# One more pair by seven products, the split ahead of the loop, the gate rows and the last norm of a two-layer fp32 encoder trunk

## The chip, the core and the metric

The kernel runs on one core of a Trainium2 chip. The metric is device microseconds of one execution, less is better; a measured kernel is run several times and its median is given. Five engines with instruction queues of their own work on it: TensorE (PE, with its weight loads as PEld), VectorE (DVE), ScalarE (ACT), GpSimd (POOL) and SyncE (SP). Here SP issues nearly all weight loads, POOL some other transfers. Each engine takes its instructions in program order; between engines they wait for semaphores.

## The reference

Two post-norm layers on x of 256 positions by 2048 columns, all in float32. The first layer mixes by a gated MLP (gMLP), the second by attention with a low-rank query and key/value; each is followed by a gated MLP with a causal convolution. What the change touches is the gMLP and the last norm:

```
def gmlp_mixer(x, w_in, ln_g, ln_b, w_s, b_s, w_out):
    z = jax.nn.gelu(x @ w_in)
    u, v = jnp.split(z, 2, axis=-1)
    v = layer_norm(v, ln_g, ln_b)
    v = v.reshape(B, S // GM_BLOCK, GM_BLOCK, GM_GROUPS, GM_GROUP_DIM)
    ...
    s = jnp.einsum('gij,bnjgd->bnigd', w, v) + jnp.transpose(b_s)[None, None, :, :, None]
    return (u * s.reshape(B, S, GM_HALF)) @ w_out
...
    for i in range(DEPTH):
        ...
        x = layer_norm(ALPHA * x + m, ln_mix_g[i], ln_mix_b[i])
        f = conv_ffn(x, ffn_w_up[i], ffn_conv_w[i], ffn_conv_b[i], ffn_w_down[i])
        x = layer_norm(ALPHA * x + f, ln_ffn_g[i], ln_ffn_b[i])
```

layer_norm is (x - mean) / sqrt(var + eps) * g + b over a row.

## The kernel before

**Products.** float32 products are made of three matmuls each (L236): an operand is split into a high part (rounded to the format fp32r) and a low part (the rest), and high x high, low x high and high x low are added up in PSUM. The x parts are split once at the start (`xhl`). A weight chunk is 128 rows (k) of 2048 columns (1 MB): SP loads it into one of three `raw` slots, ACT casts its high part `wh` (L131), DVE subtracts to get the low part `wl` (L134). The parts stand in 14 `big` slots, of which the x parts hold 6. `Feed` keeps this going: it has so many chunks split ahead of PE's use, and loads two further ones.

**Eight and seven products.** A group of outputs is 256 rows (two halves b) by 1024 columns (two halves f), in four PSUM banks. A chunk holds two k blocks of 1024 columns. Normally it takes eight products of 128x128x512, 24 matmuls (`Banks.eight`). A chunk can also be done by seven products, 21 matmuls (`Banks.seven`), as in a Strassen scheme: DVE makes sums `ts` of the chunk's quarters (L141), which are split too (`th`, `tl`), and `combine` makes sums of the x parts (`turn`, L296 to L299, then the hi cast on ACT, L307, and the lo on DVE, L308). Such a pair needs eight banks, named q3, p2, e, q4 (DIRECT) and p1, q5, p7, p6 (OWN), and five big slots instead of two. After the last pair by seven of a group, `Banks.rest()` (L447 to L451) puts the four OWN banks together: one ACT copy and four DVE additions; four more (L755) add that to DIRECT.

**Stages.** V: six groups of eight chunks, in the order V_PAIRS; V_SEVEN lists the pairs by seven. GELU follows each group, and `stats` (L713) takes squares of the result with a running sum, into throw-away tiles of the pool t2 (5 slots). Then V is normalised: the mean, variance and reciprocal root (L775 to L780, L357, L359), and `norm_v`, two DVE operations for each tile of 128x512 (L796 with g, L797 with b). The rows of g and b, called gate rows, come in by `row_v` (L788): POOL asks for a broadcast of one row from a small DRAM buffer `gbrows`, into t2 tiles `vr`, whose numbers are the group, the half and 0 for g or 1 for b. That buffer is written after group 0 from a transpose on PE (L762). U follows, six groups in the same way with banks `ub`, and the spatial product of normalised V (`spatial`, unsplit fp32 matmuls) is made between its chunks. The out-projection, the norm, the MLP, the attention layer and the last MLP come after it.

**The last norm.** The output of the last down-projection arrives in four pieces of 512 columns for each half b. `Norm.piece` adds a piece (L661 before it) and takes its statistics (L664), `start` aggregates (L669) and makes the reciprocal root (L357 on ACT, L359), and `scale` runs two DVE operations for each piece (L678: minus the mean, times g; L679: times the root, plus b) and stores it (L680).

**Order.** The Tile framework's scheduler decides the order in which each engine's instructions stand; calls marked `keep_in_program_order` keep theirs. PSUM has eight banks that are handed out in turn, and a bank or a slot is given on when its last reader is done. In `order` rows below, a tile's name ends in a running number.

Of the kernel before, what the change touches and what calls it, by code (L numbers as in the profile page):

```python
# [8 lines left out]
F32 = mybir.dt.float32  # L9
# [3 lines left out]
ALU = mybir.AluOpType  # L13
AX = mybir.AxisListType

P = 128
# [4 lines left out]
NG = 8  # L21
# [15 lines left out]
C_GMG = 0  # L37
# [11 lines left out]
V_PAIRS = [[0, 1, 2, 3, 4, 5, 6, 7]] + [[0, 2, 1, 3, 5, 4, 6, 7]] * 5  # L49
V_SEVEN = [()] + [(2, 3, 4, 6)] * 5  # L50

# [164 lines left out]
def trunk(ctx: ExitStack, tc: tile.TileContext, x, xT, gm_in, gm_wout, ffn_up, ffn_dn,  # L216
# [94 lines left out]
    for j in range(4):  # L311
        t = slot([P, 4, S], f"xraw{j}", tag="side")

        def load(q):
            nc.sync.dma_start(t[:, q, :], xT[j, :, q, :])

        def split(q):
            hi = xhl[j][:, q, 0:S]
            nc.scalar.copy(hi, t[:, q, :])
            nc.vector.tensor_tensor(xhl[j][:, q, S : 2 * S], t[:, q, :], hi.bitcast(F32), ALU.subtract)  # L320

        if j == 0:

            feed.between = [lambda: load(slice(1, 2)), lambda: split(slice(1, 2))]
            load(slice(0, 1))
            feed.ahead(1, 0)
            load(slice(2, 3))
            load(slice(3, 4))
            split(slice(0, 1))
            feed.ahead(1, 1)  # L330
            split(slice(2, 3))
            split(slice(3, 4))
        else:
            load(slice(0, 2))
            load(slice(2, 4))
            feed.ahead(2 * j, 2 * j)
            split(slice(0, 2))
            split(slice(2, 4))
        xraw.append(t)
        feed.ahead(2 * j + 2, 2 * j + 1)  # L340

# [255 lines left out]
    class Norm:  # L597
# [74 lines left out]
        def scale(self, b, f):  # L672
# [7 lines left out]
            nc.sync.dma_start(out[b * P : (b + 1) * P, c], r)  # L680

        def put(self, b, f):
            i = self.idx
# [22 lines left out]

    def stats(gi):
        if gi == 0:
            nc.vector.tensor_scalar(vc, vsum[:, :, 0], -1.0 / 512, None, op0=ALU.mult)
        for b in range(2):  # L710
            for f in range(2):
                sq = tp.tile([P, 512], F32, tag="t2", name=f"vsq{gi}{b}{f}", bufs=T2)
                nc.scalar.activation(sq, v[gi][:, b, f * 512 : (f + 1) * 512], AF.Square, bias=vc[:, b : b + 1],  # L713
                                     accum_out=vsq[:, b, 2 * gi + f : 2 * gi + f + 1])
# [5 lines left out]
    for gi in range(6):  # L720

        acc = Banks(f"v{gi}", DIRECT if gi == 0 else OWN + DIRECT if gi % 2 else DIRECT + OWN)
        rest = (None,) * 4
        for c, p in enumerate(V_PAIRS[gi]):
            a = [[x_parts(xhl, 2 * p + j, b) for j in range(2)] for b in range(2)]
            got = feed.next()
            if p in V_SEVEN[gi]:
                acc.seven(a, xc[p], *got)
                if p == V_SEVEN[gi][-1]:
                    rest = acc.rest()  # L730
            else:
                acc.eight(a, *got)
            if gi == 0 and p in V_SEVEN[1]:
                x4 = xraw[p // 2]
                room = xc_room[len(xc) // 2][:, len(xc) % 2, :]
                xc[p] = combine(p, room, x4[:, 2 * (p % 2)], x4[:, 2 * (p % 2) + 1])
            if c == 2 and gi > 0:
                stats(gi - 1)
            if c == 4 and gi == 0:
                nc.sync.dma_start(cst, consts)  # L740
# [17 lines left out]
        v.append(vt)  # L758
        if gi == 0:
            lnt, bst, gbt = bank("lnrowT"), bank("brT"), bank("gbT")  # L760
            bank("spare")
            nc.tensor.transpose(gbt[0:96, 0:P], cst[:, C_GMG : C_GMG + 96], ident)  # L762
            nc.tensor.transpose(lnt[:, 0:P], lnrow, ident)
            nc.tensor.transpose(bst[:, 0:NG], brow[0:NG, :], ident[0:NG, 0:NG])
            gbs = tp.tile([P, P], F32, tag="t1", name="gbs", bufs=T1)
            nc.scalar.copy(gbs[0:96, :], gbt[0:96, 0:P])
            nc.gpsimd.dma_start(gbd.rearrange("r (f c) -> (r f) c", c=P), gbs[0:96, :])
            nc.scalar.copy(lncol, lnt[:, 0:P])
            nc.scalar.copy(bsc, bst[:, 0:NG])
    stats(5)  # L770
    mv = [st.tile([P, 4], F32, tag="vmv", name=f"vmv{b}", bufs=2) for b in range(2)]
# [10 lines left out]

    def row_v(g, f):

        got = []
        for i in range(2):
            t = tp.tile([P, 512], F32, tag="t2", name=f"vr{g}{f}{i}", bufs=T2)
            nc.gpsimd.dma_start(t, gbd[12 * i + 2 * g + f : 12 * i + 2 * g + f + 1, :].to_broadcast([P, 512]))  # L788
            got.append(t)
        return got  # L790

    def norm_v(g, f, rows):
# [5 lines left out]

    for f, rows in enumerate([row_v(0, 0), row_v(0, 1)]):
        norm_v(0, f, rows)  # L800

    pT = [t.rearrange("p b (f c) -> p f b c", c=P) for t in v]
    acts = Acts(pT, "wo", NF_GM)
    ub = [bank(f"ub{i}") for i in range(8)]

    def spatial(g, tiles):
# [413 lines left out]
    for b in range(2):  # L1220
        for f in (2, 3):
            end(b, f)
            ln.piece(b, f, acc[b][f])
        ln.start(b)
        for f in range(4):
            ln.scale(b, f)
# [85 lines left out]
```

## Time and profile before

| | |
|---|---|
| three runs | 2468.65, 2469.26, 2470.97 us (median 2469.26) |
| the profiled execution | 2471.25 us, its span 2469.5 us |
| mean granted TensorE clock | 0.998 |
| busy in the span: PE, DVE, ACT, POOL | 2453.7, 2054.2, 1459.5, 104.2 us |
| V, U and the way between them | PE starts at 4.7 us; the first group of U has its last product at 304.6 us |
| end of the last matmul | 2459.0 us |

The page of a profile names each group of instructions by the line of the kernel, the engine, the operation, the output and its inputs, and gives counts, busy time and the idle time before them with what ended it. A timeline gives single instructions: start, duration, and in brackets the idle time of that engine before it. Matmuls are pipelined, so a row of PE lasts longer than the step from one to the next; steps are taken between starts. A row with x2 is two instructions that follow each other.

### The profile page before, as it was taken

To read this page: it belongs to the slowest core of one execution; us is meant where nothing else is said; L and a number is where in the kernel's file an instruction comes from. 1 tells how busy PE (TensorE), PEld (TensorE's weight loads), DVE (VectorE), ACT (ScalarE), POOL (GpSimd) and SP (SyncE) were. 2 spreads that over 40 slices of the span, in tenths; PEclk is the share of its full clock that TensorE was granted. 3 is DMA by queue.
4 is the path that set the end of the run, shared out by engine and by line. 5 is a ranking of instruction groups with operands and counts; after the bars stand their busy time and mean duration, and the time that the engine had idled before them with its cause. 6 is when DMAs were issued, how large, how long until landed. Compare 5 with 4: busy or idle time off the path is not lost. (4 is left out here: it accounts for less than half of the span.)

```text
span 2469.5 us, 32459 instructions
## 1 busy us (share of the span) xinstructions
PE 2453.7 (99%) x12481; PEld 2091.0 (85%) x12481; DVE 2054.2 (83%) x2734; ACT 1459.5 (59%) x1969; POOL 104.2 (4%) x202
## 2 busy tenths in 40 slices
PE   9999999999999999999999999999999999999998
PEld 7888788888888888888888888988888888888886
DVE  7999899889898788788777897867598787878798
ACT  6666565566565666556655566665565665655453
POOL 0000000000000000000000000000000000000000
PEclk9999999999999999999999999999999999999999
DMA  7555766656665678777868885544478787877885
GB/s 276 204 205 208 231 204 194 217 181 213 206 219 190 230 291 322 297 279 288 330 215 320 303 300 184 193 158 161 172 270 310 273 312 294 300 264 274 300 324 201
DMA packets 117004, 611.94 MB, mean 248 GB/s; under 512 B 10712, under 2 KB 11488, under 8 KB 75760
## 3 DMA queue, kind: packets, MB, share of 16 engines
q1 hardware_dynamic: 90704, 462.47, 52.7%
q0 software_dynamic: 26144, 147.39, 15.9%
q8 instruction: 98, 1.61, 0.3%
q14 instruction: 58, 0.48, 0.1%
HBM read 544.75 MB, written 65.06 MB: 247 GB/s over the span
## 5 line engine op out<-in xcount | busy, mean ns | idle before, releaser
L134 DVE TENSOR_TENSOR wl<-raw,wh 128x1024 fp32r<-128x1024 f32 (+4 forms) x645 | 957.3, 1499 | 176.8 <-ACT wh L131 131.8
L131 ACT CAST wh<-raw 128x1024 fp32r<-128x1024 f32 (+4 forms) x645 | 809.3, 1278 | 362.6 <-PE up L236 85.7
L236 PE MATMUL up<-xhl,wh 128*128 128x512 f32 x2624 | 611.4, 390 | 0.0
L236 PEld LDWEIGHTS up<-xhl,wh 128*128 128x128 f32 x2624 | 487.5, 188 | 97.7
L236 PEld LDWEIGHTS up<-xhl,wl 128*128 128x128 f32 x2624 | 325.8, 192 | 6.4
L236 PE MATMUL up<-xhl,wl 128*128 128x256 f32 x2624 | 328.1, 283 | 0.0
L131 ACT CAST th<-ts 128x1536 fp32r<-128x1536 f32 (+1 forms) x138 | 142.8, 1052 | 113.8 <-DVE ts L141 89.4
L236 PE MATMUL ub<-wh,xhl 128*128 128x512 f32 x576 | 179.5, 393 | 1.9 <-DVE u0w L449 1.9
L134 DVE TENSOR_TENSOR tl<-ts,th 128x1536 fp32r<-128x1536 f32 (+1 forms) x138 | 162.9, 1217 | 10.5 <-ACT th L131 3.6
L236 PEld LDWEIGHTS ub<-wh,xhl 128*128 128x128 f32 x576 | 108.1, 188 | 26.4 <-DVE u0w L449 2.4
L236 PE MATMUL ub<-wl,xhl 128*128 128x512 f32 x288 | 112.2, 389 | 0.0
L141 DVE TENSOR_TENSOR ts<-ts,raw 128x512 f32<-128x512 f32 x138 | 94.5, 684 | 1.4
L141 DVE TENSOR_TENSOR ts<-raw 128x1024 f32<-128x1024 f32 x69 | 84.0, 1218 | 7.7 <-PE ub L236 3.8
L236 PE MATMUL mo<-wh,oT 128*128 128x512 f32 x256 | 82.5, 401 | 0.0
L236 PE MATMUL v_q<-wh,xhl 128*128 128x512 f32 x224 | 70.1, 394 | 1.7 <-ACT wh L131 1.7
L236 PEld LDWEIGHTS ub<-wl,xhl 128*128 128x128 f32 x288 | 54.1, 188 | 11.4
L236 PE MATMUL v_p<-wh,xhl 128*128 128x512 f32 x192 | 60.2, 392 | 0.1
L236 PEld LDWEIGHTS v_q<-wh,xhl 128*128 128x128 f32 x224 | 42.2, 190 | 11.3 <-ACT wh L131 2.7
L236 PEld LDWEIGHTS mo<-wh,oT 128*128 128x128 f32 x256 | 45.5, 189 | 7.1
L236 PE MATMUL mo<-wl,oT 128*128 128x512 f32 x128 | 50.1, 392 | 0.0
L693 ACT ACTIVATE lny<-lnt,lncol 128x128 f32<-128x128 f32 x96 | 36.5, 469 | 15.7 <-PE lnt L689 15.6
L396 DVE TENSOR_TENSOR h_0a<-up,lo_0a 128x256 f32<-128x256 f32 x41 | 17.2, 419 | 32.7 <-ACT lo_0a L394 32.7
(1826 smaller groups left out, 4328.4 us busy)
## 6 DMA issues: line engine op xcount, KB each, us to landing
raw<-in_ffn_up_dram SPq DMA_DIRECT2D x172, 1024.0 KB, 7.1
raw<-in_gm_in_dram SPq DMA_DIRECT2D x93, 1024.0 KB, 5.3
raw<-in_ffn_dn_dram SPq DMA_DIRECT2D x68, 1024.0 KB, 6.9
raw<-in_gm_wout_dram SPq DMA_DIRECT2D x48, 1024.0 KB, 5.2
praw<-in_ffn_dn_dram POOLq DMA_DIRECT2D x16, 1024.0 KB, 15.2
keptth<-pth POOLq DMA_DIRECT2D x16, 1024.0 KB, 8.1
kepttl<-ptl POOLq DMA_DIRECT2D x16, 1024.0 KB, 9.0
fth<-keptth POOLq DMA_DIRECT2D x16, 1024.0 KB, 10.0
```

The lines of the kernel that those rows point to most:

```text
L131: cast = self.nc.scalar.copy(hi, raw)
L134: self.nc.vector.tensor_tensor(lo, raw, hi.bitcast(F32), ALU.subtract)
L141: add = lambda o, a, b: self.nc.vector.tensor_tensor(o, a, b, ALU.add)
L236: recent[0] = nc.tensor.matmul(o, l, r, start=start, stop=stop, skip_group_check=True)
L396: nc.vector.tensor_tensor(h, acc[:, 0:S], lo, ALU.add)
L693: nc.scalar.activation(y[:, j], t[:, j * P : (j + 1) * P], AF.Identity, bias=lncol[:, o : o + 1], scale=lncol[:, g : g + 1])
```

## The change

Four edits, in the order of the program:

1. Pair 6 of group 0 in V is by seven products (V_SEVEN). Six chunks are split ahead of the loop and seven loaded, instead of seven and eight. The x combinations for the pairs 2, 3, 4 and 6 are made ahead of the chunk instead of after it, 6 along with 4. Group 0 takes eight banks.
2. The three transposes (of the gate rows and of two other parameter tables) move from the end of group 0 to after the first chunk of group 1, into the bank p6 of that group.
3. The four DMAs of rows0 (g and b of the first two tiles) are issued ahead of the last `stats`, whose squares now go to PSUM banks of U that are not in use yet instead of t2 tiles.
4. The last norm of the second half has pieces 0 to 2 multiplied by g in advance (`weigh`); `finish` adds b and -mean * root * g on TensorE in three banks, by a product of ident with b and one of a diagonal matrix with g, and one DVE operation for each of these pieces remains. Piece 3 is as before.

```diff
@@ -47,7 +47,7 @@
 
 
-V_SEVEN = [()] + [(2, 3, 4, 6)] * 5
+V_SEVEN = [(6,)] + [(2, 3, 4, 6)] * 5
@@ -333,11 +333,11 @@
         else:
             load(slice(0, 2))
             load(slice(2, 4))
-            feed.ahead(2 * j, 2 * j)
+            feed.ahead(2 * j, min(2 * j, 6))
             split(slice(0, 2))
             split(slice(2, 4))
         xraw.append(t)
-        feed.ahead(2 * j + 2, 2 * j + 1)
+        feed.ahead(min(2 * j + 2, 7), min(2 * j + 1, 6))
 
@@ -679,6 +679,34 @@
             nc.vector.scalar_tensor_tensor(r, r, self.rs, self.b[:, c], ALU.mult, ALU.add)
             nc.sync.dma_start(out[b * P : (b + 1) * P, c], r)
 
+        def weigh(self, b, f):
+
+            r = self.r(b, f)
+            tc.keep_in_program_order(nc.vector.tensor_tensor(r, r, self.g[:, f * 512 : (f + 1) * 512], ALU.mult))
+
+        def finish(self, b):
+
+            t = [bank(f"fin{f}") for f in range(3)]
+            c = [slice(f * 512, (f + 1) * 512) for f in range(4)]
+            for f in range(3):
+                mm(t[f], ident, self.b[:, c[f]], True, False)
+            self.start(b)
+            pin = tc.keep_in_program_order
+            off = st.tile([P, 1], F32, tag="rstd", name="off")
+            pin(nc.vector.scalar_tensor_tensor(off, self.mu, -1.0, self.rs, ALU.mult, ALU.mult))
+            dg = tp.tile([P, P], F32, tag="t1", name="dg", bufs=T1)
+            pin(nc.vector.tensor_scalar(dg, ident, off, None, op0=ALU.mult))
+            for f in range(3):
+                mm(t[f], dg, self.g[:, c[f]], False, True)
+            r = self.r(b, 3)
+            pin(nc.vector.scalar_tensor_tensor(r, r, self.mu, self.g[:, c[3]], ALU.subtract, ALU.mult))
+            pin(nc.vector.scalar_tensor_tensor(r, r, self.rs, self.b[:, c[3]], ALU.mult, ALU.add))
+            nc.sync.dma_start(out[b * P : (b + 1) * P, c[3]], r)
+            for f in range(3):
+                r = self.r(b, f)
+                nc.vector.scalar_tensor_tensor(r, r, self.rs, t[f], ALU.mult, ALU.add)
+                nc.sync.dma_start(out[b * P : (b + 1) * P, c[f]], r)
+
@@ -704,12 +732,12 @@
     vsq = st.tile([P, 2, 12], F32, tag="vsq", name="vsq", bufs=1)
     vc = st.tile([P, 2], F32, tag="vc", name="vc", bufs=1)
 
-    def stats(gi):
+    def stats(gi, junk=None):
         if gi == 0:
             nc.vector.tensor_scalar(vc, vsum[:, :, 0], -1.0 / 512, None, op0=ALU.mult)
         for b in range(2):
             for f in range(2):
-                sq = tp.tile([P, 512], F32, tag="t2", name=f"vsq{gi}{b}{f}", bufs=T2)
+                sq = junk[2 * b + f] if junk else tp.tile([P, 512], F32, tag="t2", name=f"vsq{gi}{b}{f}", bufs=T2)
                 nc.scalar.activation(sq, v[gi][:, b, f * 512 : (f + 1) * 512], AF.Square, bias=vc[:, b : b + 1],
                                      accum_out=vsq[:, b, 2 * gi + f : 2 * gi + f + 1])
 
@@ -719,23 +747,34 @@
     gbd = dram.tile([24, 512], F32, tag="gbrows", name="gbrows", bufs=1)
     for gi in range(6):
 
-        acc = Banks(f"v{gi}", DIRECT if gi == 0 else OWN + DIRECT if gi % 2 else DIRECT + OWN)
+        acc = Banks(f"v{gi}", OWN + DIRECT if gi % 2 else DIRECT + OWN)
         rest = (None,) * 4
         for c, p in enumerate(V_PAIRS[gi]):
             a = [[x_parts(xhl, 2 * p + j, b) for j in range(2)] for b in range(2)]
             got = feed.next()
+            for p2 in V_SEVEN[1] if gi == 0 else ():
+                if p == {2: 2, 3: 3, 4: 4, 6: 4}[p2]:
+                    x4 = xraw[p2 // 2]
+                    room = xc_room[len(xc) // 2][:, len(xc) % 2, :]
+                    xc[p2] = combine(p2, room, x4[:, 2 * (p2 % 2)], x4[:, 2 * (p2 % 2) + 1])
             if p in V_SEVEN[gi]:
                 acc.seven(a, xc[p], *got)
                 if p == V_SEVEN[gi][-1]:
                     rest = acc.rest()
             else:
                 acc.eight(a, *got)
-            if gi == 0 and p in V_SEVEN[1]:
-                x4 = xraw[p // 2]
-                room = xc_room[len(xc) // 2][:, len(xc) % 2, :]
-                xc[p] = combine(p, room, x4[:, 2 * (p % 2)], x4[:, 2 * (p % 2) + 1])
             if c == 2 and gi > 0:
                 stats(gi - 1)
+            if c == 0 and gi == 1:
+                t = acc.acc["p6"]
+                nc.tensor.transpose(t[0:96, 0:P], cst[:, C_GMG : C_GMG + 96], ident)
+                nc.tensor.transpose(t[:, P : 2 * P], lnrow, ident)
+                nc.tensor.transpose(t[:, 2 * P : 2 * P + NG], brow[0:NG, :], ident[0:NG, 0:NG])
+                gbs = tp.tile([P, P], F32, tag="t1", name="gbs", bufs=T1)
+                nc.scalar.copy(gbs[0:96, :], t[0:96, 0:P])
+                nc.gpsimd.dma_start(gbd.rearrange("r (f c) -> (r f) c", c=P), gbs[0:96, :])
+                nc.scalar.copy(lncol, t[:, P : 2 * P])
+                nc.scalar.copy(bsc, t[:, 2 * P : 2 * P + NG])
...
@@ -756,18 +795,18 @@
...
-        if gi == 0:
-            lnt, bst, gbt = bank("lnrowT"), bank("brT"), bank("gbT")
-            bank("spare")
-            nc.tensor.transpose(gbt[0:96, 0:P], cst[:, C_GMG : C_GMG + 96], ident)
-            nc.tensor.transpose(lnt[:, 0:P], lnrow, ident)
-            nc.tensor.transpose(bst[:, 0:NG], brow[0:NG, :], ident[0:NG, 0:NG])
-            gbs = tp.tile([P, P], F32, tag="t1", name="gbs", bufs=T1)
-            nc.scalar.copy(gbs[0:96, :], gbt[0:96, 0:P])
-            nc.gpsimd.dma_start(gbd.rearrange("r (f c) -> (r f) c", c=P), gbs[0:96, :])
-            nc.scalar.copy(lncol, lnt[:, 0:P])
-            nc.scalar.copy(bsc, bst[:, 0:NG])
-    stats(5)
+    def row_v(g, f):
+
+        got = []
+        for i in range(2):
+            t = tp.tile([P, 512], F32, tag="t2", name=f"vr{g}{f}{i}", bufs=T2)
+            nc.gpsimd.dma_start(t, gbd[12 * i + 2 * g + f : 12 * i + 2 * g + f + 1, :].to_broadcast([P, 512]))
+            got.append(t)
+        return got
+
+    ub = [bank(f"ub{i}") for i in range(8)]
+    rows0 = [row_v(0, 0), row_v(0, 1)]
+    stats(5, ub[4:])
     mv = [st.tile([P, 4], F32, tag="vmv", name=f"vmv{b}", bufs=2) for b in range(2)]
     vrs = []
     for b in range(2):
@@ -796,13 +826,11 @@
             nc.vector.scalar_tensor_tensor(t, t, mv[b][:, 0:1], rows[0], ALU.subtract, ALU.mult)
             nc.vector.scalar_tensor_tensor(t, t, vrs[b], rows[1], ALU.mult, ALU.add)
 
-    for f, rows in enumerate([row_v(0, 0), row_v(0, 1)]):
+    for f, rows in enumerate(rows0):
         norm_v(0, f, rows)
 
...
-    ub = [bank(f"ub{i}") for i in range(8)]
-
@@ -1218,9 +1246,16 @@
     banks = [[None, None] + acc[b] for b in range(2)]
     ln, acc, end = ffn(1, ln, banks, end_mo, True)
     for b in range(2):
-        for f in (2, 3):
-            end(b, f)
-            ln.piece(b, f, acc[b][f])
+        end(b, 2)
+        ln.piece(b, 2, acc[b][2])
+        if b == 1:
+            for f in range(3):
+                ln.weigh(b, f)
+        end(b, 3)
+        ln.piece(b, 3, acc[b][3])
+        if b == 1:
+            ln.finish(b)
+            break
         ln.start(b)
         for f in range(4):
             ln.scale(b, f)
```

PE at the seventh chunk of group 0 (the last but one); wh and wl are high and low parts of the chunk, th and tl those of its sums, xc the combined x. Before:

```order
L236 MATMUL v0_q3_204<-wh6_177,xhl0_3_87 128x512 x2
L236 MATMUL v0_q3_204<-wl6_178,xhl0_3_87 128x512
L236 MATMUL v0_q3_204<-wh6_177,xhl0_3_87 128x512 x2
L236 MATMUL v0_q3_204<-wl6_178,xhl0_3_87 128x512
L236 MATMUL v0_p2_205<-wh6_177,xhl0_3_87 128x512 x2
L236 MATMUL v0_p2_205<-wl6_178,xhl0_3_87 128x512
```

and now:

```order
L236 MATMUL v0_p2_199<-wh6_319,xhl0_3_87 128x512 x2
L236 MATMUL v0_p2_199<-wl6_320,xhl0_3_87 128x512
L236 MATMUL v0_p1_202<-wh6_319,xhl0_3_87 128x512 x2
L236 MATMUL v0_p1_202<-wl6_320,xhl0_3_87 128x512
L236 MATMUL v0_q4_201<-th6_321,xhl0_3_87 128x512 x2
L236 MATMUL v0_q4_201<-tl6_322,xhl0_3_87 128x512
L236 MATMUL v0_p2_199<-wh7_376,xhl0_3_87 128x512 x2
L236 MATMUL v0_e_200<-wh7_376,xhl0_3_87 128x512
L236 MATMUL v0_q3_198<-wh6_319,xc1_89 128x512
L236 MATMUL v0_q5_203<-th6_321,xc1_89 128x512
```

The sequence of hi and lo for each product has become one in which the products of two chunks alternate.

PE where the transposes stand. Before, behind the last chunk of group 0:

```order
L236 MATMUL v0_q4_207<-wh7_355,xhl0_3_87 128x512 x2
L236 MATMUL v0_q4_207<-wl7_356,xhl0_3_87 128x512
L762 MATMUL gbT_469<-ident_186,cst_183 96x128
L763 MATMUL lnrowT_467<-ident_186,lnrow_200 128x128
L764 MATMUL brT_468<-ident_186,brow_201 128x8
L236 MATMUL v1_q3_483<-wh8_385,xhl0_0_84 128x512 x2
```

and now, in the second chunk of group 1, in its bank p6:

```order
L236 MATMUL v1_q3_496<-wh9_444,xc0_88 128x512 x2
L236 MATMUL v1_q3_496<-wl9_445,xc0_88 128x512
L770 MATMUL v1_p6_495<-ident_180,cst_177 96x128
L771 MATMUL v1_p6_495<-ident_180,lnrow_194 128x128
L772 MATMUL v1_p6_495<-ident_180,brow_195 128x8
L236 MATMUL v1_p2_497<-wh9_444,xhl0_1_85 128x512 x2
```

DVE between V and U (vr000 to vr101 are gate rows, raw and wl51 a chunk's parts of U, vmv the mean and variance, vrs the reciprocal root). Before, some of the rows:

```order
L780 TENSOR_TENSOR vmv1_2006<-vmv1_2006 128x1
L359 RECIPROCAL vrs0_2015<-vrs0q_2013 128x1
L796 SCALAR_TENSOR_TENSOR v0_462<-v0_462,vmv0_2005,vr000_2027 128x512
L797 SCALAR_TENSOR_TENSOR v0_462<-v0_462,vrs0_2015,vr001_2029 128x512
L796 SCALAR_TENSOR_TENSOR v0_462<-v0_462,vmv0_2005,vr010_2031 128x512
L797 SCALAR_TENSOR_TENSOR v0_462<-v0_462,vrs0_2015,vr011_2033 128x512
L796 SCALAR_TENSOR_TENSOR v0_462<-v0_462,vmv1_2006,vr010_2031 128x512
L134 TENSOR_TENSOR wl51_2082<-raw51_1950,wh51_2081 128x2048
L141 TENSOR_TENSOR ts52_2115<-raw52_2055 128x1024
L796 SCALAR_TENSOR_TENSOR v1_774<-v1_774,vmv0_2005,vr100_2111 128x512
L134 TENSOR_TENSOR wl52_2117<-raw52_2055,wh52_2116 128x1536
```

and now, again some:

```order
L815 TENSOR_REDUCE vmv0_2038<-vsq_192 128x1
L826 SCALAR_TENSOR_TENSOR v0_483<-v0_483,vmv0_2038,vr000_2026 128x512
L818 TENSOR_TENSOR vmv0_2038<-vmv0_2038 128x1
L826 SCALAR_TENSOR_TENSOR v0_483<-v0_483,vmv0_2038,vr010_2030 128x512
L819 TENSOR_TENSOR vmv0_2038<-vmv0_2038 128x1
L826 SCALAR_TENSOR_TENSOR v1_795<-v1_795,vmv0_2038,vr100_2128 128x512
L826 SCALAR_TENSOR_TENSOR v0_483<-v0_483,vmv1_2039,vr000_2026 128x512
L826 SCALAR_TENSOR_TENSOR v0_483<-v0_483,vmv1_2039,vr010_2030 128x512
L134 TENSOR_TENSOR wl51_2099<-raw51_1971,wh51_2098 128x2048
L826 SCALAR_TENSOR_TENSOR v1_795<-v1_795,vmv1_2039,vr100_2128 128x512
L827 SCALAR_TENSOR_TENSOR v0_483<-v0_483,vrs0_2048,vr001_2028 128x512
L141 TENSOR_TENSOR ts52_2132<-raw52_2072 128x1024
```

The first operations with g for the halves of the first two tiles (L826, was L796) have moved up between the operations on the variance, and vr100's first use stands ahead of wl51; before, wl51 stood ahead of it.

DVE at the end of the program, in the last norm of the second half (lnmv is the mean and variance, lnrs the root, lng and lnb g and b, dn11_q4 the bank of the last piece, fin0 to fin2 the new banks). Before:

```order
L664 BN_STATS lnst3_1_19367<-res3_1_20724 128x6
L661 TENSOR_TENSOR res3_1_20724<-res3_1_20724,dn11_q4_20199 128x512
L664 BN_STATS lnst3_1_19367<-res3_1_20724 128x6
L669 BN_AGGR lnmv3_1_21011<-lnst3_1_19367 128x2
L678 SCALAR_TENSOR_TENSOR res3_0_19894<-res3_0_19894,lnmv3_1_21011,lng3_20772 128x512
L359 RECIPROCAL lnrs3_1_21015<-lnrs3_1q_21013 128x1
L678 SCALAR_TENSOR_TENSOR res3_0_19894<-res3_0_19894,lnmv3_1_21011,lng3_20772 128x512
L679 SCALAR_TENSOR_TENSOR res3_0_19894<-res3_0_19894,lnrs3_1_21015,lnb3_20774 128x512 x2
L678 SCALAR_TENSOR_TENSOR res3_1_20724<-res3_1_20724,lnmv3_1_21011,lng3_20772 128x512 x2
L679 SCALAR_TENSOR_TENSOR res3_1_20724<-res3_1_20724,lnrs3_1_21015,lnb3_20774 128x512 x2
```

and now, without the last L664:

```order
L685 TENSOR_TENSOR res3_0_19911<-res3_0_19911,lng3_20789 128x512 x2
L685 TENSOR_TENSOR res3_1_20741<-res3_1_20741,lng3_20789 128x512
L661 TENSOR_TENSOR res3_1_20741<-res3_1_20741,dn11_q4_20216 128x512
L669 BN_AGGR lnmv3_1_21037<-lnst3_1_19384 128x2
L359 RECIPROCAL lnrs3_1_21041<-lnrs3_1q_21039 128x1
L696 SCALAR_TENSOR_TENSOR off_21043<-lnmv3_1_21037,lnrs3_1_21041 128x1
L698 TENSOR_SCALAR dg_21045<-ident_180,off_21043 128x128
L702 SCALAR_TENSOR_TENSOR res3_1_20741<-res3_1_20741,lnmv3_1_21037,lng3_20789 128x512
L703 SCALAR_TENSOR_TENSOR res3_1_20741<-res3_1_20741,lnrs3_1_21041,lnb3_20791 128x512
L707 SCALAR_TENSOR_TENSOR res3_0_19911<-res3_0_19911,lnrs3_1_21041,fin0_21031 128x512
L707 SCALAR_TENSOR_TENSOR res3_0_19911<-res3_0_19911,lnrs3_1_21041,fin1_21032 128x512
L707 SCALAR_TENSOR_TENSOR res3_1_20741<-res3_1_20741,lnrs3_1_21041,fin2_21033 128x512
```

Of the eight operations behind the aggregate two stand as before, for piece 3 (L702, L703), three are one each with a bank (L707), and three (L685) stand ahead of the last addition L661.

More of the change, by code (lines that the diff above doesn't have):

```diff
@@ L781, in trunk @@
         vrs.append(rstd_of(mv[b][:, 1:2], 0, f"vrs{b}"))
[L783 to L790, printed above, removed]
     def norm_v(g, f, rows):
```

## The prediction

> **What bounds the kernel now.** I read the page first: busy times, then the chain that ended last.
>
> ```profile
> span 2469.5 us, 32459 instructions
> PE 2453.7 (99%) x12481; PEld 2091.0 (85%) x12481; DVE 2054.2 (83%) x2734; ACT 1459.5 (59%) x1969; POOL 104.2 (4%) x202
> PE 34%; DVE 0%; DVEq 0%; issue 0%
> ```
>
> TensorE is busy 2453.7 of 2469.5 us, so only 15.8 us of the span are not matmuls, and the rest falls only if matmuls go. The next two views say where the 15.8 us lie: PE's waits, and windows (columns here: width, then busy us and count of PE, PEld, DVE, ACT, POOL; then the granted clock, the DMA share and GB/s).
>
> ```profile
> PE ub L236 <- DVE u0w L449: 1.9, 1, 1.9
> PE v_q L236 <- ACT wh L131: 1.7, 1, 1.7
> 54.00:255.00 201.00, 201.00 (x889) 166.48 (x888) 192.68 (x173) 134.05 (x164) 2.93 (x8) 1.00 0.59 208
> 255.00:310.00 55.00, 52.99 (x229) 42.66 (x228) 48.29 (x64) 32.08 (x43) 4.82 (x9) 1.00 0.71 226
> 2455.00:2470.00 15.00, 4.03 (x18) 3.00 (x16) 8.77 (x15) 0.29 (x1) 0.00 (x0) 0.77 0.32 122
> ```
>
> From 54 to 255 us PE never stops. From 255 to 310 it loses 2.0 us, nearly all of it one wait for u0w. After 2455 it has 4.0 us of work in 15: the last norm, 11 us in which nothing multiplies. The 1.7 us wait for the first hi chunk at the start is not touched. The change can therefore win in three places: fewer matmuls in group 0, the wait near 305, the tail. I cost them in that order.
>
> **Group 0: three matmuls fewer.** Start times of PE rows, eight products:
>
> ```profile
> 42.00 0.62 PE L236 MATMUL v_q<-wh,xhl 128*128 128x512 f32 x2
> 47.44 0.62 PE L236 MATMUL v_q<-wh,xhl 128*128 128x512 f32 x2
> 52.89 0.27 PE L762 MATMUL gbT<-ident,cst 128*96 128x128 f32 x1
> 53.35 0.73 PE L236 MATMUL v_q<-wh,xhl 128*128 128x512 f32 x2
> ```
>
> A chunk of 24 matmuls takes 47.44 - 42.00 = 5.44 us, 0.2267 us each. Pair 6 by seven products has 21: 3 x 0.2267 = **-0.68 us**. The three transposes (52.89 to 53.35, 0.46 us) are moved, not removed: nothing.
>
> What it adds lies on DVE and ACT. The chunk needs sums (ts), a second hi/lo pair (th, tl) and a combined x part, and at its end four additions and an ACT copy in rest().
>
> ```profile
> 40.19 4.49 DVE L134 TENSOR_TENSOR wl<-raw,wh 128x2048 fp32r<-128x2048 f32 x2 [1.10 <-ACT wh L131]
> 44.60 0.28 DVE L296 TENSOR_TENSOR xs<-xraw 128x128 f32<-128x128 f32 x1
> 51.08 1.76 DVE L134 TENSOR_TENSOR wl<-raw,wh 128x1536 fp32r<-128x1536 f32 x1 [4.34 <-ACT wh L131]
> ```
>
> DVE waits 4.34 us before 51.08, so it has room. With steps of 2.2 us for a 2048-wide lo ((44.60 - 40.19) / 2), 1.7 for 1536 columns, 1.15 for the long sum and 0.6 for 512 columns (305.08 to 306.83 below) I walked the new order from 30.5 us: the second chunk's hi cast ends near 42.9 against 44.0 where PE asks for it, its lo 45.1 against 46.3, the combined part's lo 45.8 against 47.0. Cover is about 1.1 us each; if it is gone, PE waits by the shortfall. The tightest place comes later. The transposes now stand in PE's queue behind the second chunk of group 1, in a bank of that group, and wait for DVE's addition that empties it, which stands behind the four of rest(). My walk has it done at 57.8; PE comes at 58.3. Behind the transposes all PE work queues. Price: 0 if the walk holds, up to 2 us (three more 0.6-us additions late) if not; I take 0.
>
> **V to U: the gate rows.** These rows carry the term: POOL's issues of the rows, DVE, and PE.
>
> ```profile
> 259.57 1.06 POOL L788 DMA_DIRECT2D vr<-gbrows  x2 [198.74 <-ACT vsq L713]
> 261.55 0.54 POOL L788 DMA_DIRECT2D vr<-gbrows  x1 [0.91 <-ACT vsq L713]
> 258.36 0.68 DVE L755 TENSOR_TENSOR v<-v_q,v5u 128x512 f32<-128x512 f32 x1
> 269.73 0.75 DVE L796 SCALAR_TENSOR_TENSOR v<-v,vmv,vr 128x512 f32<-128x512 f32 x1 [3.03 <-DMA vr<-gbrows]
> 295.64 6.70 DVE L134 TENSOR_TENSOR wl<-raw,wh 128x2048 fp32r<-128x2048 f32 x3
> 305.08 1.22 DVE L141 TENSOR_TENSOR ts<-raw 128x1024 f32<-128x1024 f32 x1 [2.15 <-DMA raw<-in_gm_in_dram]
> 306.23 0.68 DVE L449 TENSOR_TENSOR u0w<-ub,u0u 128x512 f32<-128x512 f32 x1
> 294.98 0.61 PE L236 MATMUL ub<-th,xhl 128*128 128x512 f32 x2
> 295.66 0.50 PE L236 MATMUL ub<-tl,xhl 128*128 128x512 f32 x1
> 296.00 0.63 PE L236 MATMUL ub<-th,xc 128*128 128x512 f32 x2
> 304.64 0.39 PE L236 MATMUL ub<-wl,xhl 128*128 128x512 f32 x1
> 306.97 0.73 PE L236 MATMUL ub<-wh,xhl 128*128 128x512 f32 x2 [1.94 <-DVE u0w L449]
> ```
>
> Read backwards. PE should go on at 304.87 and goes at 306.97: 2.10 us. It waits for u0w, which stood behind a sum whose chunk landed late, because its slot came free only with the lo of 295.64. DVE was that late because it lost 3.03 us before 269.73, waiting for a gate row. At 294.98 three matmuls take until 296.00, 1.02 us instead of 3 x 0.2267 = 0.68: another 0.34, a tl that is late for the same reason. Together **2.44 us** to win.
>
> Now the rows wait only for five t2 slots, which the additions of 255.4 to 258.4 leave: I put the five issues at 256.4 to 259.6, the third 3.3 us sooner. When do they land? DMA's queues (0 is POOL's, 1 is SP's: packets, MB, share of 16 engines) in 256 to 260.3, 260.9 to 265, 265 to 267 and 267 to 271:
>
> ```profile
> q1 hardware_dynamic: 336, 1.28, 95.4%
> ...
> q0 software_dynamic: 149, 0.50, 72.7%
> ...
> q1 hardware_dynamic: 146, 0.60, 89.9%
> q0 software_dynamic: 6, 0.00, 1.4%
> ...
> q0 software_dynamic: 314, 1.05, 70.9%
> ```
>
> Until 260.3 the engines carry older weights. Then two rows pass in 4.1 us (2.0 each); then the weights asked for at 261.4 go first, and four rows follow in 267 to 271 at 70.9% (0.7 each). Asked for before 261.4, all five come ahead of those weights: the fifth lands at 260.3 + 5 x 0.7 = 263.9 to 260.3 + 5 x 2.0 = 270.3; I take the middle, **T = 267**. The fifth counts, because the new DVE order has its first use ahead of the next weight's lo. Adding the DVE durations down the new order, the tl of the third U chunk by seven is ready at T + 18.8, and PE asks for it at 285.24 in the trace: T may be 266.4. The first spatial matmul allows 267.3, u0w (ready T + 36.4 to T + 38.5, wanted at 304.87) 266.4 or later. So PE loses T - 266.4 = 0.6 us instead of 2.44: **-1.84 us**; bounds -2.44 (T up to 266.4) and +1.5 (T = 270.3). Three transfers are moved ahead of one SP load; POOL has nothing else queued there. The squares of stats(5) now go to PSUM; the target can change them by tenths, on an ACT that is 32 of 55 us busy: nothing.
>
> **The tail.** DVE rows of the last block:
>
> ```profile
> 2459.07 0.69 DVE L661 TENSOR_TENSOR res<-res,dn_q 128x512 f32<-128x512 f32 x1 [2.35 <-PE dn_q L236]
> 2460.81 0.75 DVE L678 SCALAR_TENSOR_TENSOR res<-res,lnmv,lng 128x512 f32<-128x512 f32 x1
> 2461.48 0.16 DVE L359 RECIPROCAL lnrs<-lnrs_1q 128x1 f32<-128x1 f32 x1
> 2464.85 1.41 DVE L679 SCALAR_TENSOR_TENSOR res<-res,lnrs,lnb 128x512 f32<-128x512 f32 x2
> 273.81 3.60 PE L236 MATMUL ub<-v,wT 128*128 128x512 f32 x12
> 277.06 0.81 PE L236 MATMUL ub<-wh,xhl 128*128 128x512 f32 x2
> ```
>
> Before, eight 0.66-us operations follow the aggregate, the last ending at 2466.26. Now three multiplications by g (3 x 0.61) go into the 2.35 us that DVE waits before 2459.07: hidden, with 0.5 to spare. Behind the aggregate, the reciprocal no longer queues behind an L678 and starts near 2461.14; off and dg end at about 2461.75, two operations for piece 3 end at 2463.1, three with PSUM operands (0.66 to 0.7 each) bring the end to 2465.2 if their banks are ready. An unsplit fp32 matmul of 128x512 costs (277.06 - 273.81) / 4 = 0.81 us. Three for b run while PE is idle, 2458.9 to 2461.3; three for g from 2461.8 end by 2464.3, and the last DVE operation starts at 2464.5. So 2466.26 - 2465.2 = **-1.0 us**; bounds -1.2 and +1.3. The latter is PE at half clock (only 0.77 was granted after 2455): the last three would take 1.6 us each, 2461.8 to 2466.7, and the last operation end near 2467.5. The 256-KB stores behind are as many as before.
>
> **Sum.** -0.68 - 1.84 - 1.0 = -3.5 us on the profiled execution's span of 2469.5; that execution took 2471.25, the median of the three runs is 2469.26. On the median: **2465.8 us**.
>
> **Rivals.** *Everything comes off (0.28):* T up to 266.4 and the tail at 1.2 make 0.68 + 2.44 + 1.2 = 4.3 us, 2464.9; a few tenths of what I do not see pass the bound below. For it: the 0.7-us rows. Against: the first two took 2.0.
>
> *The rows get stuck (0.12), the other side:* if the weights of 261.4 are let in between the rows, and the rows go at 2.0 each, T = 260.3 + 10 + 3.5 (1 MB at the rate of 265 to 267) = 273.8, PE loses 7.4 us, and 2469.26 - 0.68 - 1.0 - 2.44 + 7.4 = 2472.5. DVE stands in order, so a late fifth row now holds up the weights' lo parts, which in the old order went past it. It is slower than before from T = 270.5 on. For it: the 72.7% row; against: in 265 to 267 the queues took turns load by load, and the rows now stand ahead. The Trainium skill, "DMA: Bandwidth & Descriptors", section "Queues, rings and completion order", has each engine go round the rows of queues and drain a whole packet from one before switching; by that the weights would cut in after one gate row, which is this rival's first half. The 1.4% beside 89.9% agrees with whole loads at a time but does not show who goes first.
>
> *Group 0 stalls (0.10):* the transposes wait some 2 us for their bank, or the second hi cast is late: 2465.8 + 2 = 2467.8. A wait can also cost the clock: after the 1.7-us wait of the start the matmuls step by 0.43 instead of 0.23,
>
> ```profile
> 10.45 0.63 PE L236 MATMUL v_p<-wh,xhl 128*128 128x512 f32 x1
> 10.88 0.63 PE L236 MATMUL v_q<-wl,xhl 128*128 128x512 f32 x1
> ```
>
> for 3.4 us, 1.7 us more: 2469.5. Against: behind the 1.94-us wait at 306.97 they step at full speed.
>
> *The tail gives nothing (0.10):* the half clock above, or the PSUM operands wait: 2466.8, or 2468.1 by the bound. The likeliest case keeps 0.40, with 2464.4 to 2467.0 as its own range.
>
> **How the numbers follow.** 0.2%, 4.9 us, is about what a measurement of this kernel can tell from no change: faster is below 2464.3, slower above 2474.2. All named gains at their best come to 4.3 us, so faster needs the first rival and tenths more: 0.17 of its 0.28, and 0.03 from the others by chance, 0.20. Slower needs T beyond 275 or two rivals at once: 0.06. Within: 0.74. The range, 2464.2 to 2469.5, leaves out the far end of the stuck rows and what lies beyond all gains.
>
> **What would show it.** Group 0: 21 matmuls for pair 6, no idle PE ahead of the transposes near 58. V to U: the first row asked for near 256.4, the fifth landed by 267, no PE wait near 304. Tail: from the start of the last L661 to the end of the last DVE operation 6.1 us, where it was 2466.26 - 2459.07 = 7.2. I am wrong if PE waits for v normalised near 273, if the rows land past 270, or if the last three matmuls end after the DVE operation of piece 3 by more than 1.4 us.

## The result

The changed kernel takes 2466.98 us (median of 20 runs, 2465.39 to 2468.60); the kernel before takes 2470.74 us (20 runs, 2468.65 to 2472.71). The ratio is 0.9986, 95% interval 0.998 to 0.9992: faster by 3.8 us, between 2.0 and 4.9. That is inside the forecast range and inside "within 0.2%". The profiled execution took 2466.91 us, its span 2465.1.

The page of the changed kernel, span and busy times, then PE's waits (total, times, longest):

```profile
span 2465.1 us, 32504 instructions
PE 2457.0 (100%) x12490; PEld 2090.4 (85%) x12490; DVE 2061.6 (84%) x2749; ACT 1461.8 (59%) x1972; POOL 104.2 (4%) x202
PE v_q L236 <- ACT wh L131: 0.9, 1, 0.9
PE v_p L236 <- ACT wh L131: 0.7, 2, 0.5
PE ub L236 <- DVE u0w L449: 0.5, 1, 0.5
PE fin L236 <- DVE dg L698: 0.3, 1, 0.3
```

The wait for u0w has shrunk from 1.9 to 0.5 us, but has not gone; the wait for a hi cast (L131) into a p bank appears twice, and only one of the two is at the start. Three places have to be read one by one.

**Group 0.** PE, ACT and DVE of the changed kernel (start, duration, instruction, idle time before):

```profile
41.10 0.62 PE L236 MATMUL v_q<-th,xhl 128*128 128x512 f32 x2
41.55 0.39 PE L236 MATMUL v_q<-tl,xhl 128*128 128x512 f32 x1
42.16 0.73 PE L236 MATMUL v_p<-wh,xhl 128*128 128x512 f32 x2 [0.22 <-ACT wh L131]
...
39.68 0.62 ACT L307 CAST xc<-xs 128x512 fp32r<-128x512 f32 x1 [3.54 <-PE v_q L236]
40.20 1.91 ACT L131 CAST wh<-raw 128x2048 fp32r<-128x2048 f32 x1
...
39.28 0.49 DVE L299 TENSOR_TENSOR xs<-xraw,xs 128x128 f32<-128x128 f32 x2
```

The products with the second chunk's hi part should start at 41.78 (one step of 0.2267 after 41.55) and start at 42.16; the next step is 0.11 too long. PE waits because the cast of 40.20 ends at 42.11. ACT had been idle for 3.54 us, but a cast of a combined x part (L307) stood ahead of it. The bracket blames PE; but of DVE's last two additions for the x parts (L299; two parts are combined in turn), the first, from 39.28 on, ends at 39.57, 0.11 us ahead of that cast. In the kernel `g0` the step is the same 0.11 us, and the same wait reads "<-DVE xs L299". The transposes at 56.66 waited for nothing.

**V to U.** DVE and PE of the changed kernel:

```profile
253.87 0.54 POOL L803 DMA_DIRECT2D vr<-gbrows  x1 [191.08 <-issue]
255.07 2.18 POOL L803 DMA_DIRECT2D vr<-gbrows  x4 [0.67 <-DVE v L794]
260.14 0.75 DVE L826 SCALAR_TENSOR_TENSOR v<-v,vmv,vr 128x512 f32<-128x512 f32 x1 [0.99 <-DMA vr<-gbrows]
262.89 0.75 DVE L826 SCALAR_TENSOR_TENSOR v<-v,vmv,vr 128x512 f32<-128x512 f32 x1 [1.93 <-DMA vr<-gbrows]
264.84 0.75 DVE L826 SCALAR_TENSOR_TENSOR v<-v,vmv,vr 128x512 f32<-128x512 f32 x1 [1.05 <-DMA vr<-gbrows]
302.64 0.68 DVE L449 TENSOR_TENSOR u0w<-ub,u0u 128x512 f32<-128x512 f32 x1
303.38 0.73 PE L236 MATMUL ub<-wh,xhl 128*128 128x512 f32 x2 [0.55 <-DVE u0w L449]
```

U's first product starts at 255.14 here and at 257.49 before, so times are compared from there. The five rows are asked for at -1.3 to +1.6 us (before: +2.1 to +5.5), and the first use of the fifth is at 264.84 - 255.14 = 9.7. DVE still waits 4.0 us for rows (0.99 + 1.93 + 1.05) where it waited 3.03 for one; what changed is that this waiting ends earlier.

**The tail.**

```profile
2455.45 0.69 DVE L661 TENSOR_TENSOR res<-res,dn_q 128x512 f32<-128x512 f32 x1 [0.56 <-PE dn_q L236]
2457.53 0.16 DVE L359 RECIPROCAL lnrs<-lnrs_1q 128x1 f32<-128x1 f32 x1 [0.36 <-ACT lnrs_1q L357]
2458.91 0.75 DVE L703 SCALAR_TENSOR_TENSOR res<-res,lnrs,lnb 128x512 f32<-128x512 f32 x1
2459.57 2.32 DVE L707 SCALAR_TENSOR_TENSOR res<-res,lnrs,fin 128x512 f32<-128x512 f32 x3
2458.26 2.84 PE L236 MATMUL fin<-lng,dg 128*128 128x512 f32 x6 [0.27 <-DVE dg L698]
```

From the last L661 to DVE's end: 2459.57 + 2.32 - 2455.45 = 6.44 us, before 7.19. The last product ends at 2461.10, 1.44 us behind the end of piece 3 (L703, 2459.66).

**A table by stage.** The same marks in the trace of every kernel: the start of the 97th product matmul, of U's first, of the one 11000 before the last of dn_q (in U's second group), of the last of dn_q, and the end of the span. Each column is the difference of two marks, in us; the first is the 97th matmul's start itself. T is the first use of the fifth gate row, from U's start. The kernels are described below. (The 4.7 us given earlier for PE's start is that of the last dummy matmul; the first product of that profile starts at 4.99.)

| kernel | 97th at | to U | U's first stretch | to last dn_q | tail | T |
|---|---|---|---|---|---|---|
| before | 31.12 | 226.37 | 88.37 | 2112.78 | 10.84 | |
| before2 | 30.15 | 226.37 | 88.35 | 2112.76 | 10.85 | |
| changed | 28.86 | 226.28 | 87.13 | 2112.75 | 10.12 | 9.69 |
| after2 | 29.11 | 226.40 | 86.24 | 2113.10 | 10.10 | 8.96 |
| g0 | 30.33 | 225.83 | 87.73 | 2112.75 | 10.85 | |
| rows | 28.75 | 226.37 | 86.14 | 2112.92 | 10.84 | 9.19 |
| tail | 29.16 | 226.37 | 88.41 | 2112.85 | 10.11 | |
| rowstail | 30.41 | 226.37 | 85.79 | 2112.78 | 10.10 | 8.31 |
| comb | 29.43 | 225.93 | 85.88 | 2112.88 | 10.11 | 8.32 |
| comb2 | 31.32 | 225.89 | 85.89 | 2113.31 | 10.11 | 8.07 |
| warm | 28.99 | 227.76 | 86.10 | 2112.81 | 10.10 | 8.82 |
| combwarm | 29.82 | 225.93 | 85.87 | 2112.91 | 10.12 | 8.51 |
| fewrows | 30.03 | 226.49 | 85.77 | 2112.93 | 10.10 | 7.52 |

Read by rows: the two executions of the kernel before agree to 0.02 us in every stretch but the first, which differs by 1.0. Of the 4.3 us between the two first spans, 2.3 lie ahead of the 97th matmul, where the change takes no matmul away (edit 1 has one chunk less split and loaded ahead there).

### The profile page after: what moved, and what is told of

Read it like the earlier page. It is cut to its first block, busy times and chain, and to the rows that moved or that the text cites. A ratio compares the mean times of both kernels' runs of the same rounds, so it can differ in the third digit from the quotient of the medians.

```text
span 2465.1 us, 32504 instructions
## 1 busy us (share of the span) xinstructions
PE 2457.0 (100%) x12490; PEld 2090.4 (85%) x12490; DVE 2061.6 (84%) x2749; ACT 1461.8 (59%) x1972; POOL 104.2 (4%) x202
## 5 line engine op out<-in xcount | busy, mean ns | idle before, releaser
L131 ACT CAST wh<-raw 128x1024 fp32r<-128x1024 f32 (+4 forms) x645 | 809.1, 1277 | 346.0 <-PE up L236 85.3
L131 ACT CAST th<-ts 128x1536 fp32r<-128x1536 f32 (+1 forms) x140 | 145.1, 1051 | 124.8 <-DVE ts L141 103.2
L236 PEld LDWEIGHTS v_q<-wh,xhl 128*128 128x128 f32 x216 | 40.4, 188 | 10.2 <-ACT wh L131 1.9
```

Of the source, the lines that this page charges most:

```text
L131: cast = self.nc.scalar.copy(hi, raw)
L236: recent[0] = nc.tensor.matmul(o, l, r, start=start, stop=stop, skip_group_check=True)
```

## The experiments

**Each edit alone, and the whole again.** Edits 1 and 2 (`g0`), 3 (`rows`) and 4 (`tail`) were put on the kernel before, each as in the diff above; `after2` is the changed kernel unaltered. All times are beside 33 runs of the kernel before on the same chip (median 2470.25).

> Edits 1 and 2 alone (pair 6 of group 0 by seven products, six chunks split ahead, transposes moved). Theory A (the three places are independent, and the 2.3 us that lie ahead of 36 us between the two profiles belong to the start of an execution, not to the change): the time falls by 0.1 to 0.7 us; in the profile PE has 21 matmuls for pair 6, and where its start is early (second chunk's products at 8.3 us) it waits some 0.5 us near 42 for a hi cast; the wait for u0w near 305 stays near 2 us. Rival B (the earlier start comes with the change, by way of edit 1, which alters the work ahead of the loop): the time falls by 2.5 to 3 us and the profile is some 2.3 us ahead at 36 us.

Measured: 2469.38 us, ratio 0.9998 (0.9989 to 1.0007): 0.9 us less, a little more than theory A has, far within the interval. No wait near 42 us, and V is 0.54 us shorter. But this was an execution whose start ran at half clock (97th matmul at 30.33): ACT's cast ended at 43.03 and PE asked at 43.26. The wait for u0w was 1.7 us. As for rival B, a gain of 2.5 us lies at the edge of the interval, and this profile is not ahead at the start.

> Edit 3 alone (gate rows asked for ahead of the last stats, squares to PSUM). Theory A: the time falls by 1.0 to 2.0 us; all between 255 and 310 us, the wait for u0w shrinks from 2.1 us to 0.5 to 1.0, and DVE waits three times for a gate row, some 4 us in all. Rival C (the remaining lateness near 303 comes from edit 1 having moved PE forward, not from the rows): alone, the rows take the waits of 2.44 us away altogether and the time falls by 2.4.

Measured: 2468.01 us, ratio 0.9993 (0.9984 to 1.0002); U's first stretch is 2.2 us shorter, the other stretches are the same to 0.15. PE's wait near 303 shrank to 0.16 us, less than theory A asked for; DVE's three waits are there, 3.1 us in all. Rival C is nearer in its number, but kernels with edit 1 and no wait (`comb`, `combwarm`) show below that it is T that decides, and T moves from execution to execution.

> Edit 4 alone (last norm helped by TensorE). Theory A: from the start of the last L661 to the end of the last DVE operation 6.4 us instead of 7.2, and the time falls by 0.8 us. Rival D (the tail is worth 1.0 as costed, and a late start of the second piece in the changed kernel was particular to that execution): 6.1 to 6.2 us.

Measured: 2468.67 us, ratio 0.9995 (0.9986 to 1.0004). 6.44 us, as in the changed kernel, and the tail 0.73 us shorter. Theory A; rival D falls.

> The changed kernel once more, for a second profile and for its time beside the parts. Theory A: the time falls by 2.1 to 3.8 us, about the sum of the three parts; the start of the execution (where the second weight piece's products begin, and at what clock) may be either of the two that the first two profiles show. Rival B: the start is the early one again, and the wait near 42 us is there again.

Measured: 2466.53 us, ratio 0.9987 (0.9978 to 0.9995). The wait near 42 us is there again (0.63 us with the long step behind it), V has gained nothing, U's first stretch 2.1 us. The single edits' medians add up to 0.9 + 2.2 + 1.6 = 4.7 us and the whole gives 3.7: each of these has an interval of some 2 us either way, so this sum tells nothing; the stages do.

**What PE waits for near 42 us.** `comb` is the changed kernel with the pairs combined in another order. It and the three kernels after it are beside another 33 runs of the kernel before (median 2469.45).

```diff
-            for p2 in V_SEVEN[1] if gi == 0 else ():
-                if p == {2: 2, 3: 3, 4: 4, 6: 4}[p2]:
+            for p2 in (6, 2, 3, 4) if gi == 0 else ():
+                if p == {6: 3, 2: 4, 3: 5, 4: 6}[p2]:
```

> The changed kernel with the x combination of pair 6 made first (ahead of those of pairs 2, 3 and 4, which now come later), so that nothing that waits for DVE stands ahead of the second chunk's hi cast on ACT. Theory E (the wait of 0.5 to 0.6 us near 42 comes from that cast, which stood on ACT behind the cast of a combined x part): no PE wait from 30 to 50 us even where the start is early, and from the 97th matmul to the first of U 225.7 us (226.37 less 0.68) instead of 226.3 to 226.4; the time 0.5 us below the changed kernel's. Rival F (the slot of the cast comes free only by PE's own progress, so the cast would be as late anyway): the wait stays, 226.3.

ACT of this kernel:

```profile
33.72 1.49 ACT L131 CAST th<-ts 128x1536 fp32r<-128x1536 f32 x1 [0.54 <-DVE ts L141]
35.11 1.91 ACT L131 CAST wh<-raw 128x2048 fp32r<-128x2048 f32 x1
36.92 0.61 ACT L131 CAST th<-ts 128x512 fp32r<-128x512 f32 x1
41.00 0.62 ACT L307 CAST xc<-xs 128x512 fp32r<-128x512 f32 x1 [3.46 <-DVE xs L299]
```

The second chunk's hi cast now runs at 35.11, five us earlier, ahead of the cast that waits for DVE; its slot was free by then, and rival F falls. No PE wait is left there. V takes 225.93 us, 0.44 less than before instead of 0.68: of what is missing, 0.11 is a long step near 207, the rest is spread over steps too small to name. The time is 2466.00 us, ratio 0.9987 (0.9978 to 0.9995), where `warm` has 2467.21 and `fewrows` 2467.01 beside the same runs of the kernel before; both have the wait. The intervals overlap.

**What the start does.** `warm` is the changed kernel with more dummy matmuls, `combwarm` has this and the edit of `comb`:

```diff
-    for _ in range(9):
+    for _ in range(12):
         mm(warm, idle[:, 0:P], idle, True, True)
```

> The changed kernel with 12 instead of 9 dummy matmuls ahead of the first product; nothing else. Theory G (the 2.3 us that profiles of the same start differ by are the landing of the first pieces and, in some executions, half clock for 3.4 us after PE's wait near 7 to 9 us): PE's first product starts 1.2 us later, its waits before 9 us shrink by as much, no half clock behind 9 us, the 97th matmul at 28.6 to 29.2 us, and the median falls by 0.3 to 0.8 us with less spread. Rival H (the half clock comes in windows that do not care about 2 us more or less): the same spread, and the median the same or up to 1 us more.

Measured: 2467.21 us (2465.23 to 2468.97), ratio 0.9989 (0.998 to 0.9997): nothing gained, and no less spread. No half clock behind 9 us and the 97th matmul at 28.99, as theory G says; but the changed kernel has it at 28.86 and 29.11, so this profile won nothing there, and near 43.8 PE lost 1.87 us to the very cast above. For the time this run does not separate G from H.

> Both of the last edits, the earlier combination of pair 6 and 12 dummy matmuls. Theories E and G: about 1 us below the changed kernel, 4.5 to 5 us below the kernel before. Rivals F and H: as the changed kernel.

Measured: 2465.83 us, ratio 0.9985 (0.9976 to 0.9994), 11 runs from 2465.05 to 2466.42. The best of all, but not told apart from `comb`. All 11 runs have a granted clock of 1.000; of the 22 of `comb` and `comb2` (below), four have 0.998 or 0.999, and these are the four longest (2467.62 to 2468.71, the others at most 2466.48). Eleven runs without such a one are too few to put it down to the dummy matmuls.

**Whether the gate rows are what is late.** `fewrows` leaves out the rows of the second tile and uses those of the first. POOL still asks for five rows at once, but the one whose use is T is now the third of them:

```diff
-    rows0 = [row_v(0, 0), row_v(0, 1)]
+    rows0 = [row_v(0, 0)] * 2
```

> The changed kernel with the g and b rows of the first tile used for the second one too: two of the first five row transfers are left out, and the second tile is normalised with the wrong rows. Theory A (what PE still loses in U's first group is set by when the fifth gate row's use starts, T, by T + 38.5 - 47.4 us after U's start): T falls from 9.0 to 9.7 us after U's start to about 7, no PE wait for u0w, U's first stretch 85.9 to 86.1 us instead of 86.2 to 87.1; the time 0.2 to 0.9 us below the changed kernel's. Rival I (the weights of U, not the rows, are late by then): the wait near 303 stays at 0.3 to 0.7 us.

Measured: 2467.01 us, ratio 0.9988 (0.9979 to 0.9997); T = 7.5 and no wait for u0w, U's first stretch 85.77. Rival I falls. The gain in the time could not be seen beside the spread of the start and the wait of 0.6 us near 43.5. The table's column T says it with more rows: PE's loss ahead of u0w is 0.71 us at T = 9.69, 0.16 at 9.19, 0.30 at 8.96, 0.19 at 8.82, and none at 8.51 and below. Two of these are out of order, so T settles the loss only to some 0.2 us. The three profiles with pair 6 combined first (`comb`, `combwarm`, `comb2`) have T at 8.51 or less, `changed`, `after2` and `warm` at 8.82 or more; whether that is the order or chance is not shown.

**The change without edits 1 and 2**, `rowstail`, the kernel before again, and `comb` again, beside 27 runs of the kernel before (median 2469.69):

> Edits 3 and 4 without 1 and 2: group 0 as in the kernel before, transposes at its end. Theory J (edit 1 as written gives nothing, because PE waits 0.5 to 0.6 us for the second chunk's hi cast what the three matmuls save): the time is that of the changed kernel within 0.3 us, 3.0 us below the kernel before (2.23 for the rows, 0.73 for the tail); from the 97th matmul to U 226.37 us, U's first stretch 86.1 to 86.4. Rival K (edit 1 gives 0.5 us or more, by the start or by fewer waits in U): 0.5 to 1.2 us above the changed kernel.

Measured: 2467.20 us, ratio 0.9989 (0.9981 to 0.9998). By stages as J says: 226.37, and U's first stretch even 85.79. By the ratio it is 0.5 to 0.7 us above the changed kernel (0.9986 and 0.9987), the edge between J and K and far within the interval.

> The kernel before once more, for a second profile. Theory G, first half (the start differs between executions whatever the kernel): from the first product to the 97th matmul 23.7 to 26.1 us, as likely short as long; the other stretches 226.4, 88.4, 2112.8 and 10.84 us to 0.1. Rival B (an early start comes with the change alone): again 26 us, half clock behind 9 us.

Measured: 2469.25 us, ratio 0.9999 (0.999 to 1.0008). The stretches are as expected; the start took 25.4 us and again had half clock, here up to 10.6 us. That alone would leave B alive; `comb2` settles it.

> The changed kernel with pair 6 combined first, once more, beside the two others. Theory E: 225.9 us from the 97th matmul to U, no wait near 42 us, and 0.4 to 0.6 us below the kernel without edits 1 and 2; about 3.5 us below the kernel before.

Measured: 2465.91 us, ratio 0.9986 (0.9977 to 0.9995); 225.89, no wait near 42; 1.3 us below `rowstail` by the medians, more than expected and within the spread. Its profiled execution, like `before`, started late, with the 97th matmul at 31.32, where the same kernel as `comb` had it at 29.43. The start differs by 1.9 us within one kernel; two profiles of kernels with edit 1 (`g0`, `comb2`) started late, two without it (`rows`, `tail`) early. Rival B falls.

## Why the prediction came out as it did

The forecast was -3.5 us, the median moved by 3.8. Step by step it is less good than that.

- **Group 0, -0.68 us: the step that failed.** The three matmuls are gone, but V is 0.09 us shorter in one profile and 0.03 longer in the other. The walk down the order put the second chunk's hi cast at 42.9 with 1.1 us of cover. With the 97th matmul as mark, which starts 2.26 us earlier here, PE asked at 41.78 + 2.26 = 44.0 in the clock of the profile before, as forecast, and the cast ended at 42.11 + 2.26 = 44.4. The cast was put 1.5 us too early. It stood on ACT behind the cast of a combined x part, which waits for DVE; with that one moved behind it, in `comb` and `comb2`, the wait is gone. The walk gives no time for the cast ahead, so how much of the 1.5 us is DVE's work stays open. From profile to profile the place moves: the cast was 0.2 us ahead of PE in `g0` and cost 1.87 us in `warm`. That is the rival "group 0 stalls", with a quarter to a third of its price (0.49 and 0.63 us). The place called tightest, the transposes, held.
- **V to U, -1.84 us.** The chain was right: T was forecast at 267, 9.5 us after U's start, and came at 9.69 and 8.96; the limit was put at 8.9 and lies between 8.5 and 8.8. U's first stretch became 1.24 and 2.13 us shorter, either side of the term. The stuck rows did not happen. That T came so near is in part luck: 267 was the middle of a range of 6.4 us, and the rows took a course that the sum does not have, most of them fast and the last packets late (the views below).
- **The tail, -1.0 us.** Right in kind, off in size: -0.73. Up to the first L707 it went as costed (4.12 us after the last L661, forecast 4.0). Then the three products took 2.84 us (forecast 3 x 0.81 = 2.43), the last of the three L707 started only when the third bank was done (2461.14), and the three took 2.32 us instead of 2.0 to 2.1. So one of the prediction's signs of being wrong came, just: the last product ended 1.44 us behind the DVE operation of piece 3, where 1.4 was the limit.
- **The sum.** The stages of the two profiles give on average 0.0 - 1.7 - 0.7 = -2.4 us, in the interval (-2.0 to -4.9) but 1.3 short of the median's 3.8. The marks do not divide this rest: ahead of the 97th matmul the executions of one kernel spread over 1.9 us, U's first stretch of the changed kernel over 0.9, and there are two profiles of it. Whether the start comes late less often in the changed kernel stays open: it takes many profiles of each. So the forecast's closeness is in part luck: one term gave nothing, another a quarter less, and a rest that no term names made up for it. What the stages show is the 2.4.

The Trainium skill's rule in the prediction ("DMA: Bandwidth & Descriptors", "Queues, rings and completion order") can be weighed with the rows of the changed kernel in 257 to 261 and in 262 to 264, with weights asked for at 258.7:

```profile
q0 software_dynamic: 325, 1.09, 75.9%
q1 hardware_dynamic: 99, 0.34, 22.9%
...
q1 hardware_dynamic: 179, 0.72, 94.8%
q0 software_dynamic: 14, 0.04, 5.3%
```

Of five rows (1.3 MB), 1.1 MB passed before those weights began; the last packets trailed beside them until 264, and the fifth row was first used at 264.84. The weights did not cut in after one row, and no delay of 3.5 us is seen; that the last packets trail beside them fits turns that are taken, as the rule has it, but no run took the weights away to show it.

## What to carry to other kernels

A product saved on the busiest engine is worth what the engines that feed it can keep up with: look for what stands ahead of the feeding instruction in its own queue, since an in-order engine that idles 3.5 us can still be the one that is late. Moving work that was not needed yet behind the feeding instruction won 0.4 of the 0.7 us that the saved matmuls had promised. With changes of some 0.1%, marks in the trace, from stage to stage, tell apart what eleven runs of the whole time cannot.

## What was not expected of the hardware

The half clock at the start does not follow the length of PE's wait. In every profile the first dummy matmuls step by 0.43 us, where later ones step by 0.2267. PE of `before2`, with a wait of 0.77 us, and of `after2`, with 1.43 us:

```profile
4.78 1.42 PE L236 MATMUL v_q<-wh,xhl 128*128 128x512 f32 x2
6.96 0.79 PE L236 MATMUL v_p<-wh,xhl 128*128 128x512 f32 x1 [0.77 <-ACT wh L131]
7.55 0.63 PE L236 MATMUL v_q<-wl,xhl 128*128 128x512 f32 x1
7.97 0.63 PE L236 MATMUL v_p<-wh,xhl 128*128 128x512 f32 x1
...
4.78 1.30 PE L236 MATMUL v_q<-wh,xhl 128*128 128x512 f32 x2
7.51 0.51 PE L236 MATMUL v_p<-wh,xhl 128*128 128x512 f32 x1 [1.43 <-ACT wh L131]
7.85 0.40 PE L236 MATMUL v_q<-wl,xhl 128*128 128x512 f32 x1
8.09 0.40 PE L236 MATMUL v_p<-wh,xhl 128*128 128x512 f32 x1
```

`before2` goes on at the dummies' step of 0.43 us up to 10.6: its wait did not slow it, its clock had not risen yet. `after2` steps by 0.23 to 0.24 at once. Of the 13 profiles five have half clock behind 9 us, and in two different ways. In `before2`, `g0` and `rowstail` no matmul is faster than the dummies before 10.2 us. In `before` and `comb2` the step was already 0.24 and is 0.43 again from 9.00 and 9.42 to about 12.3, behind waits of 1.72 us and of 1.85 and 0.41 us. The other eight keep the full step once they have it, all by 7.3 us, `fewrows` through waits of 1.45 and 1.03 us. The granted clock shows only the second way: for 10 to 20 us it is 0.88 in `before` and `comb2`, but 1.00 in `before2` and `g0`, and 1.00 too for their first 10 us, in which everything steps by 0.43.

The Trainium skill, "TensorE: Matmul & The Clock Gate", section "Part 1: The HAM clock gate (the "warmup" mystery)", has the clock fall after at least one idle window of about 3.4 us, the windows running freely. The free running would fit the chance in it; an idle stretch of 3.4 us none of these executions had there.
